# GpSimd makes the lo parts of the activations at four exchanges

## The chip, the core and the metric

The kernel runs on one core of a Trainium2 chip. Its time is that of one execution on the device, in microseconds (us). Four compute engines matter: TensorE (PE: matrix products, with PEld for its weight loads), VectorE (DVE), ScalarE (ACT) and GpSimd (POOL). SyncE (SP) issues the transfers between the chip's main memory and the on-chip memory SBUF. Results of TensorE stand in PSUM.

## The reference

One layer of a streaming encoder over 512 tokens of width 2048, all in float32:

```
h = rms_norm(x, norm_mix)
b, c, v = split(h @ conv_w_in, 3);  u = c * v
x = x + (b * conv3(u)) @ conv_w_out
h = rms_norm(x, norm_mlp)
a = relu(h @ mlp_w1)                # 2048 -> 8192
out = x + (a * a) @ mlp_w2          # 8192 -> 2048
```

The change concerns the last line, (a * a) @ mlp_w2, called the second MLP product here.

## The kernel before, in words

**Exactness.** TensorE multiplies in a shorter float format (fp32r). To keep float32 accuracy every operand is cut in two: hi is the operand rounded to fp32r, lo is the operand minus hi. A product is the sum of three: hi by hi, hi by lo, lo by hi (lines 267 to 269). `split` (lines 118 to 121) makes the parts: ScalarE copies to hi, VectorE subtracts to get lo.

**Fewer products.** Nearly all products run through `fast` (line 243), a scheme with seven products of half-size blocks instead of eight (Strassen's scheme in Winograd's form). The weights of a block of 256 output columns are cut into four quarters, from which VectorE makes four sums (line 179). The activations are likewise held as seven forms: quarters Y11, Y12 or T1, Y21, Y22 in `quart`, two of the sums T2 and T4 in `sums`, and T3 in `last_sum`. Each form is 128 partitions by 2048 elements in its hi and in its lo part.

**Steps.** A block of 256 columns is seven steps, one for each product, in the order X11, S1, S2, S4, S3, X12, X22; each has 24 matmuls (8 times 3). The order of instructions on all engines is written out by hand (lines 635 to 651): in turn i come the matmuls of step i, then `out` of step i-1 (it adds the bank to the result in c: on VectorE at line 279 for S4, S3 and X12, on ScalarE at line 281 otherwise), the weight sums of step i+3, the split of the weights of step i+2 into whi and wlo (three buffers each), and last whatever `at` has put down for that turn. Every engine works through its own list in this order, and waits where something is not ready.

**The second MLP product.** The 8192 rows of mlp_w2 are taken in four chunks of 2048. For each chunk eight blocks of 256 columns are computed, and each result c is added to a running sum x_mid (`add_up`, line 357 on VectorE, two turns after the block).

**Exchanges.** A chunk has its own seven forms of the activation, computed earlier and kept in main memory as `hidden`. They have to replace the old ones in SBUF while the last block of the work before still uses them. `exchange` (lines 343 to 350) does it during that block and the next: `fetch` (line 302) loads form i into one of three buffers f (tag q), `settle` (line 305) splits f into the hi and lo part of the form. With s the block's first step, the forms are settled in turns s+2, s+3, s+4, s+6, s+9, s+10 and s+11, and first used in steps s+7 to s+13:

```
for i in range(7):
    at(start + reads[i], fetch, box, src, i)
for i, t in enumerate((2, 3, 4, 6, 9, 10, 11)):
    at(start + t, settle, box, i)
```

There are four exchanges, hence 28 calls of `settle` in them: the first in the last block of the first MLP product, where the same buffers also serve `squared_relu` (lines 193 and 435 on VectorE), the others between the chunks. `settle` is also called elsewhere, at `pass_over` and once at the end of the mixer (lines 320 to 341 and 612).

**SP's list.** All loads are issued by SyncE in the same order. Between the fetches of an exchange stand the four loads of a weight block (line 146) and the loads and stores of x_mid. A fetch that waits for a free buffer holds up what is behind it.

GpSimd has nothing to do in the whole kernel but a few constants at the start.

Of the kernel before, what the change touches and what calls it, by code (L numbers as in the profile page):

```python
# [8 lines left out]
F32 = mybir.dt.float32  # L9
# [3 lines left out]
ALU = mybir.AluOpType  # L13
# [26 lines left out]
def trunk_kernel(  # L40
# [12 lines left out]
    nc = tc.nc  # L53
    x, out = x[0], out[0]
    w_in, w_out = conv_w_in[0], conv_w_out[0]
    w1, w2 = mlp_w1[0], mlp_w2[0]
    act, dve, pe = nc.scalar, nc.vector, nc.tensor
# [49 lines left out]
    def form(i):  # L107
        if i == T3:
            return last_sum
        return [quart[n][:, HOME[i]] if i in HOME else sums[n][:, i == T4] for n in range(2)]  # L110

    def gain(which, kt):
        return par[:, which * KT + kt : which * KT + kt + 1]
# [1 line left out]
    def tap(i, kt):  # L115
        return par[:, (2 + i) * KT + kt : (2 + i) * KT + kt + 1]

    def split(hi, lo, src):

        act.copy(hi, src)  # L120
        dve.tensor_tensor(out=lo, in0=src, in1=hi.bitcast(F32), op=ALU.subtract)  # L121

    def bank():
        return psum.tile([P, S], F32, tag="acc", name="acc")
# [24 lines left out]
    def operand(src, shape):  # L149
        hi = wp.tile(shape, F32R, tag="whi", name="whi", bufs=RING)  # L150
        lo = wp.tile(shape, F32R, tag="wlo", name="wlo", bufs=RING)
        split(hi, lo, src)
        return hi, lo
# [49 lines left out]
    def at(i, fn, *args):  # L203
        between.setdefault(i, []).append((fn, args))
# [15 lines left out]
    def plain(w, r0, c0):  # L220
        box = new_block(w, r0, c0, KT // QK)

        def multiply(op, k0):
            if k0 == 0:
                box["acc"] = [bank() for _ in range(2)]
            plain_products(box["acc"], op, k0, k_first=True)

        def out(k0):
            if k0 == KT - QK:
                c = tile_c(box)  # L230
                for j in range(2):
                    act.copy(c[:, j, :], box["acc"][j])

        for k0 in range(0, KT, QK):
            steps.append((
                lambda: None,
                lambda k0=k0: plain_operand(box["r"], k0),
                lambda op, k0=k0: multiply(op, k0),
                lambda k0=k0: out(k0),
            ))  # L240
        return box
# [59 lines left out]
        box[i] = tile_q("f")  # L301
        nc.sync.dma_start(box[i], src[:, :, PLACE[i], :].rearrange("k p t -> p k t"))

    def settle(box, i):
        split(*form(i), box.pop(i))

    def fetch_pairs(box, src, k, n):

# [4 lines left out]
    def settle_pairs(box, k, n):  # L313
        f = box.pop(k).rearrange("p (k q) t -> p q k t", q=4)[:, :, :n, :]
        split(*(quart[i][:, :, k : k + n, :] for i in range(2)), f)
# [4 lines left out]
    def pass_over(last, first, src):  # L320


        s, f, box = last["start"], first["start"], {}
        at(s - 2, fetch_pairs, box, src, 0, 2)
        at(s, fetch_pairs, box, src, 2, 2)
        at(s + 1, settle_pairs, box, 0, 2)
        at(s + 1, fetch_pairs, box, src, 4, 2)
        at(s + 2, settle_pairs, box, 2, 2)
        at(s + 3, settle_pairs, box, 4, 2)
        at(s + 3, fetch_pairs, box, src, 6, 1)  # L330
        at(f, settle_pairs, box, 6, 1)
        at(f, settle_last, last)
        box = {}
        at(f + 1, fetch, box, src, T2)
        at(f + 2, fetch, box, src, T3)
        at(f + 3, settle, box, T2)
        at(f + 3, fetch, box, src, T1)
        at(f + 3, settle, box, T3)
        at(f + 3, fetch, box, src, T4)
        at(f + 4, settle, box, T1)  # L340
        at(f + 6, settle, box, T4)

    def exchange(start, src, reads):


        box = {}
        for i in range(7):
            at(start + reads[i], fetch, box, src, i)
        for i, t in enumerate((2, 3, 4, 6, 9, 10, 11)):
            at(start + t, settle, box, i)  # L350


    wide = lambda t: t.unsqueeze(1).to_broadcast([P, 2, S])
# [121 lines left out]
    with tc.tile_pool(name="xin", bufs=2) as xin:  # L475
# [18 lines left out]
        for c in range(D // XC):  # L494
# [5 lines left out]
            for i in range(2):  # L500
                src = w_in[c * XC : (c + 1) * XC, parts[i] : parts[i] + GC]
# [3 lines left out]
            for j in range(0, XK, 2):  # L505
                xs = xin.tile([P, 2, S], F32, tag="xs", name="xs")
                for i in range(2):
                    kt = c * XK + j + i
                    pt = bank()
                    for b in range(S // P):  # L510
# [3 lines left out]
                    hi, lo = (quart[n][:, 2 * i : 2 * i + 2, kt // 2, :] for n in range(2))  # L514
# [3 lines left out]
                        out=lo, in0=pt, scalar=gain(0, kt), in1=hi.bitcast(F32),  # L518
# [83 lines left out]
    for n in range(NG):  # L602
        if n in (0, NG - 1):
            box = plain(w_out, 0, n * GC)
        else:
            box = fast(w_out, 0, n * GC, late=n == 1)
# [9 lines left out]
    for n in range(DFF // GC):  # L616
        last, box = box, fast(w1, 0, n * GC, late=n == 1) if n else plain(w1, 0, n * GC)
        if n == 0:
            pass_over(last, box, normed)
            at(box["start"] + 2, token_factors, lambda name: tile_x(name)[:, 0, :S])  # L620
        if n == DFF // GC - 1:
            exchange(box["start"], hidden[0], (-2, -1, 2, 3, 4, 5, 6))
        squared_relu(n, box)
    for ch in range(NCH):
        if ch:
            exchange(box["start"], hidden[ch], (-2, -1, 0, 2, 3, 4, 6))
        for n in range(NG):
            box = fast(w2, ch * D, n * GC)
            add_up(ch, n, box)
# [52 lines left out]
```

## Time and profile before

| what | us |
|---|---|
| median of 3 runs (lowest, highest) | 2005.88 (2002.95, 2007.34) |
| the profiled execution's own time | 2005.84 |
| its span, first to last instruction | 2004.1 |
| TensorE busy in the span | 1932.6 |
| VectorE busy | 1650.9 |
| ScalarE busy | 979.5 |
| GpSimd busy | 0.7 |

The mean granted clock of TensorE is 0.985 of full speed. Matmuls overlap, so that TensorE's busy time says only where it rests. A group row of the profile reads: line, engine, operation, output<-inputs, shapes, count, then the busy time in us, the mean ns of one, and the idle time of the engine just before them with what ended it. A timeline row reads: start in us from the span's start, length in us, engine, line, operation, operands, and in brackets the idle time before it with what released it.

### The profile page before, as it was taken

What the parts mean: (1) busy time and instruction counts of PE and PEld (TensorE: products, weight loads), DVE (VectorE), ACT (ScalarE), POOL (GpSimd) and SP (SyncE); (2) the same over time, 40 slices, a digit from 0 to 9 for tenths busy, and PEclk for the clock granted to TensorE, in tenths of its full rate; (3) what the DMA queues carried; (4) which work ended last, traced back from release to release, by engine and by line L of the source; (5) the groups of instructions that cost most, each with busy time, mean ns of one, the idle gap of its engine ahead of it and who ended that gap; (6) DMA issues with size and microseconds to landing.
All of it is one profiled execution on the core that took longest, in us unless ns stands there. A gap on an engine that the chain in (4) does not pass through costs nothing. (4 is left out here: it accounts for less than half of the span.)

```text
span 2004.1 us, 36810 instructions
## 1 busy us (share of the span) xinstructions
PE 1932.6 (96%) x15729; PEld 1886.7 (94%) x15729; DVE 1650.9 (82%) x1686; ACT 979.5 (49%) x1232; POOL 0.7 (0%) x6
## 2 busy tenths in 40 slices
PE   9979999999989989999999999988999999999998
PEld 7769999999789879999999999988998998999998
DVE  6678988887688778888888888888889789879776
ACT  4544444444455544444544445454455446446443
POOL 0000000000000000000000000000000000000000
PEclk9999999999989989999999999999999999999999
DMA  8433433434755855445354453575556457548432
GB/s 273 168 126 112 142 130 103 148 106 170 266 184 198 306 177 171 152 165 180 136 190 152 164 181 135 190 250 177 183 198 243 159 188 265 178 149 291 161 136 96
DMA packets 279843, 355.79 MB, mean 178 GB/s; under 512 B 9520, under 2 KB 253312, under 8 KB 273536
## 3 DMA queue, kind: packets, MB, share of 16 engines
q1 hardware_dynamic: 279552, 353.41, 50.8%
q8 instruction: 123, 2.02, 0.4%
q14 instruction: 40, 0.33, 0.0%
q10 hardware_dynamic: 128, 0.04, 0.0%
HBM read 277.91 MB, written 75.50 MB: 176 GB/s over the span
## 5 line engine op out<-in xcount | busy, mean ns | idle before, releaser
L267 PE MATMUL acc<-q_hi,whi 128*128 128x256 f32 x2816 | 781.3, 277 | 4.0 <-ACT c L281 4.0
L269 PE MATMUL acc<-q_hi,wlo 128*128 128x256 f32 x2816 | 780.2, 277 | 2.6 <-DVE wlo L121 2.6
L268 PE MATMUL acc<-q_lo,whi 128*128 128x256 f32 x2816 | 780.5, 277 | 1.0 <-DVE q_lo L121 1.0
L121 DVE TENSOR_TENSOR wlo<-r,whi 128x1024 fp32r<-128x1024 f32 x384 | 469.2, 1222 | 232.2 <-ACT whi L120 222.6
L267 PEld LDWEIGHTS acc<-q_hi,whi 128*128 128x128 f32 x2816 | 531.1, 189 | 4.3 <-ACT c L281 4.2
L269 PEld LDWEIGHTS acc<-q_hi,wlo 128*128 128x128 f32 x2816 | 530.1, 188 | 3.1 <-DVE wlo L121 3.0
L268 PEld LDWEIGHTS acc<-q_lo,whi 128*128 128x128 f32 x2816 | 530.6, 188 | 1.9 <-DVE q_lo L121 1.8
L120 ACT CAST whi<-r 128x1024 fp32r<-128x1024 f32 x384 | 401.0, 1053 | 212.6 <-PE acc L268 115.8
L267 PE MATMUL acc<-t_hi,whi 128*128 128x256 f32 x1408 | 397.4, 282 | 32.8 <-DVE c L279 21.8
L269 PE MATMUL acc<-t_hi,wlo 128*128 128x256 f32 x1408 | 395.6, 281 | 2.2 <-DVE wlo L121 2.2
L268 PE MATMUL acc<-t_lo,whi 128*128 128x256 f32 x1408 | 395.5, 281 | 0.0
L120 ACT CAST whi<-s 128x1024 fp32r<-128x1024 f32 x264 | 278.4, 1055 | 206.0 <-DVE s L179 143.6
L121 DVE TENSOR_TENSOR wlo<-s,whi 128x1024 fp32r<-128x1024 f32 x264 | 322.3, 1221 | 25.9 <-ACT whi L120 22.2
L281 ACT COPY c<-acc 128x256 f32<-128x256 f32 x352 | 130.3, 370 | 402.2 <-PE acc L269 386.7
L267 PEld LDWEIGHTS acc<-t_hi,whi 128*128 128x128 f32 x1408 | 271.4, 193 | 35.1 <-issue 23.3
L269 PEld LDWEIGHTS acc<-t_hi,wlo 128*128 128x128 f32 x1408 | 270.9, 192 | 2.4 <-DVE wlo L121 2.4
L268 PEld LDWEIGHTS acc<-t_lo,whi 128*128 128x128 f32 x1408 | 271.1, 193 | 0.0
L267 PE MATMUL acc<-u_hi,whi 128*128 128x256 f32 x704 | 203.7, 289 | 13.5 <-ACT c L281 13.5
L268 PE MATMUL acc<-u_lo,whi 128*128 128x256 f32 x704 | 201.4, 286 | 1.3 <-DVE u_lo L121 1.3
L269 PE MATMUL acc<-u_hi,wlo 128*128 128x256 f32 x704 | 201.4, 286 | 0.0
L267 PEld LDWEIGHTS acc<-u_hi,whi 128*128 128x128 f32 x704 | 136.9, 195 | 14.7 <-ACT c L281 14.7
L268 PEld LDWEIGHTS acc<-u_lo,whi 128*128 128x128 f32 x704 | 137.0, 195 | 2.0 <-DVE u_lo L121 2.0
(76 smaller groups left out, 1796.7 us busy)
## 6 DMA issues: line engine op xcount, KB each, us to landing
r<-in_mlp_w_dram SPq DMA_DIRECT2D x256, 512.0 KB, 6.2
r<-in_conv_w_in_dram SPq DMA_DIRECT2D x96, 512.0 KB, 6.2
hidden<-q SPq DMA_DIRECT2D x32, 1024.0 KB, 4.3
f<-hidden SPq DMA_DIRECT2D x28, 1024.0 KB, 8.4
r<-in_conv_w_out_dram SPq DMA_DIRECT2D x32, 512.0 KB, 6.4
xt<-x_mid SPq DMA_DIRECT2D x32, 512.0 KB, 8.8
x_mid<-c SPq DMA_DIRECT2D x24, 512.0 KB, 2.6
gated<-q SPq DMA_DIRECT2D x8, 1024.0 KB, 3.8
```

Source lines behind the costliest of these rows:

```text
L120: act.copy(hi, src)
L121: dve.tensor_tensor(out=lo, in0=src, in1=hi.bitcast(F32), op=ALU.subtract)
L267: pe.matmul(acc, hi[:, k, :], f_hi[:, k, :], start=first, stop=False, skip_group_check=True)
L268: pe.matmul(acc, hi[:, k, :], f_lo[:, k, :], start=False, stop=False, skip_group_check=True)
L269: pe.matmul(acc, lo[:, k, :], f_hi[:, k, :], start=False, stop=last, skip_group_check=True)
L281: act.copy(o, acc)
```

## The change

`split` gets an argument that names the engine of the subtraction, VectorE where nothing is said; `settle` passes it on; and `exchange`, alone of the callers, passes GpSimd. ScalarE's copy to hi stays, the fetches stay, and so do all turns.

```diff
-    def split(hi, lo, src):
+    def split(hi, lo, src, rest=dve):
 
         act.copy(hi, src)
-        dve.tensor_tensor(out=lo, in0=src, in1=hi.bitcast(F32), op=ALU.subtract)
+        rest.tensor_tensor(out=lo, in0=src, in1=hi.bitcast(F32), op=ALU.subtract)
...
-    def settle(box, i):
-        split(*form(i), box.pop(i))
+    def settle(box, i, rest=dve):
+        split(*form(i), box.pop(i), rest)
...
         for i, t in enumerate((2, 3, 4, 6, 9, 10, 11)):
-            at(start + t, settle, box, i)
+            at(start + t, settle, box, i, nc.gpsimd)
```

The 28 subtractions of 128 by 2048 elements leave VectorE's list and form GpSimd's. The buffer f is free again when GpSimd's subtraction has ended, and TensorE's products with the lo part wait for GpSimd.

## The prediction

> **What bounds the kernel now.** I read the page first, for which engine is full, then stretches of the span, to compare the exchanges with ordinary work, and then the groups, the timeline and the DMA issues inside one exchange.
>
> ```profile
> PE 1932.6 (96%) x15729; PEld 1886.7 (94%) x15729; DVE 1650.9 (82%) x1686; ACT 979.5 (49%) x1232; POOL 0.7 (0%) x6
> ```
>
> TensorE is the bound of the whole; VectorE (DVE) is next. Below, columns are: length, busy time (count) of PE, PEld, DVE, ACT, POOL, granted clock, DMA share, GB/s.
>
> ```profile
> 1799.00:1818.10 19.10, 19.10 (x169) 19.10 (x168) 15.34 (x16) 9.64 (x12) 0.00 (x0) 1.00 0.77 267
> 1829.00:1833.30 4.30, 4.30 (x24) 4.30 (x25) 4.30 (x5) 2.86 (x2) 0.00 (x0) 0.63 1.09 387
> ```
>
> The first row is an ordinary stretch, about one block of seven steps: TensorE never rests, DVE needs 15.34 of 19.10 us, GpSimd does nothing. The second is explained below.
>
> ```profile
> 1322.00:1369.00 47.00, 33.86 (x248) 32.89 (x247) 38.75 (x35) 26.07 (x24) 0.00 (x0) 0.88 0.71 241
> 1493.00:1534.00 41.00, 36.32 (x295) 35.58 (x295) 39.22 (x33) 26.73 (x26) 0.00 (x0) 0.96 0.84 291
> 1654.00:1695.00 41.00, 36.62 (x300) 35.88 (x299) 39.47 (x33) 26.61 (x26) 0.00 (x0) 0.96 0.84 292
> 1815.00:1856.00 41.00, 36.96 (x298) 36.22 (x298) 39.44 (x33) 26.76 (x26) 0.00 (x0) 0.96 0.84 291
> ```
>
> These hold the four exchanges. TensorE is idle 13.1, 4.7, 4.4 and 4.0 us of them, and DVE is nearly full in the last three, which are alike. I work with the fourth. Its DVE groups, from the first lo part to the last (1819.30 to 1852.05):
>
> ```profile
> L121 DVE TENSOR_TENSOR q_lo<-f,q_hi 128x2048 fp32r<-128x2048 f32 x4 | 9.1, 2284 | 0.0
> L121 DVE TENSOR_TENSOR wlo<-r,whi 128x1024 fp32r<-128x1024 f32 x6 | 7.3, 1218 | 0.1
> L121 DVE TENSOR_TENSOR t_lo<-f,t_hi 128x2048 fp32r<-128x2048 f32 x2 | 4.6, 2284 | 0.0
> L121 DVE TENSOR_TENSOR wlo<-s,whi 128x1024 fp32r<-128x1024 f32 x3 | 3.7, 1219 | 0.0
> L357 DVE TENSOR_TENSOR c<-c,xt 128x1024 f32<-128x1024 f32 x2 | 2.4, 1219 | 0.0
> L121 DVE TENSOR_TENSOR u_lo<-f,u_hi 128x2048 fp32r<-128x2048 f32 x1 | 2.3, 2284 | 0.0
> L279 DVE TENSOR_TENSOR c<-acc,c 128x256 f32<-128x256 f32 x5 | 2.1, 417 | 0.0
> L179 DVE TENSOR_TENSOR r<-r 128x1024 f32<-128x1024 f32 x1 | 1.2, 1218 | 0.0
> L179 DVE TENSOR_TENSOR s<-r,s 128x1024 f32<-128x1024 f32 x1 | 1.2, 1217 | 0.0
> L179 DVE TENSOR_TENSOR s<-s,r 128x1024 f32<-128x1024 f32 x1 | 1.2, 1216 | 0.0
> L179 DVE TENSOR_TENSOR s<-r 128x1024 f32<-128x1024 f32 x1 | 1.2, 1215 | 0.0
> ```
>
> Idle before them is 0.1 us in all: DVE sets the pace for these 33 us. The timeline shows that instructions overlap by some 0.08 us, and what TensorE waits for:
>
> ```profile
> 1819.23 2.29 DVE L121 TENSOR_TENSOR q_lo<-f,q_hi 128x2048 fp32r<-128x2048 f32 x1
> 1821.43 1.22 DVE L121 TENSOR_TENSOR wlo<-r,whi 128x1024 fp32r<-128x1024 f32 x1
> 1822.57 2.29 DVE L121 TENSOR_TENSOR q_lo<-f,q_hi 128x2048 fp32r<-128x2048 f32 x1
> ...
> 1849.83 2.28 DVE L121 TENSOR_TENSOR t_lo<-f,t_hi 128x2048 fp32r<-128x2048 f32 x1
> 1852.03 0.42 DVE L279 TENSOR_TENSOR c<-acc,c 128x256 f32<-128x256 f32 x1
> ```
> ```profile
> 1829.00 0.55 PE L267 MATMUL acc<-t_hi,whi 128*128 128x256 f32 x1 [2.40 <-DVE c L279]
> 1852.59 0.36 PE L267 MATMUL acc<-t_hi,whi 128*128 128x256 f32 x1 [1.20 <-DVE c L279]
> ```
>
> Start to start, a lo part takes 2.20 us of DVE (1819.23 to 1821.43), a weight operand 1.14 (1821.43 to 1822.57). Twice TensorE stands because the short addition of line 279 sits behind a lo part. After the 2.40 us gap the clock is down: 0.63 over 4.30 us in the row above, so 4.30 x 0.37 = 1.6 us more.
>
> **The change, part by part.** *Removed from DVE:* 28 lo parts, seven per exchange, 7 x 2.20 = 15.4 us each time, with DVE the pace. If nothing came in their place, the fourth exchange would need 32.8 - 15.4 = 17.4 us of DVE, less than TensorE's own work there, and the losses would go.
>
> *Added to GpSimd:* the same 28, 128x2048 with two inputs from SBUF. No row shows one. The nearest:
>
> ```profile
> masks.py:199 POOL TENSOR_SCALAR_AFFINE_SELECT ident<-ident 128x128 f32<-128x128 f32 x1 | 0.3, 292 | 0.1
> ...
> L668 POOL MEMSET const-float32-0.0<- 128x1 f32 x1 | 0.1, 98 | 0.2 <-issue 0.2
> ```
>
> With 98 ns fixed, one tensor read costs GpSimd (292 - 98)/128 = 1.52 ns an element, so 2048 take 3.2 us with one input and, if the inputs are read in turn, 6.3 with two. Below, DVE's 2.3 is the floor. I take X = 4.7, between one and two inputs, and keep 3.2 and 6.3. The Trainium skill, GPSIMD Engine Reference, section 3.1, states 4497 ns for just this operation at this size; the sum would then be 2059 us; no run shows it yet.
>
> *What hides it.* Seven in a row on GpSimd take 7 x 4.7 = 32.9 us, from the end of the first hi part on:
>
> ```profile
> 1816.81 1.91 ACT L120 CAST q_hi<-f 128x2048 fp32r<-128x2048 f32 x1
> ...
> 1848.10 1.05 ACT L120 CAST whi<-r 128x1024 fp32r<-128x1024 f32 x1
> ```
>
> That is 1818.7 to 1851.6, against 1852.1 for the last lo part now. So even with DVE untouched the last lo part comes hardly earlier: the chain moves from DVE to GpSimd, which lags behind the steps set for a DVE twice as fast. Behind a waiting GpSimd instruction only further lo parts are queued, and TensorE waits for them.
>
> *Moved: the release of f.* Three buffers serve seven fetches, and the fourth fetch starts as the first lo part ends:
>
> ```profile
> 1821.54 0.36 SPq L302 DMA_DIRECT2D f<-hidden  x1
> ...
> 1828.96 4.61 SPq L146 DMA_DIRECT2D r<-in_mlp_w_dram  x4
> ```
> ```profile
> f<-hidden SPq DMA_DIRECT2D x4, 1024.0 KB, 6.7
> r<-in_mlp_w_dram SPq DMA_DIRECT2D x8, 512.0 KB, 7.8
> ```
>
> Landing 6.7, hi part 1.9 and lo part 4.7 make 13.3 us for three, under GpSimd's own 14.1: the fetches stay hidden. Behind the sixth fetch on SP's queue stand four weight loads; the third release moves from 1828.5 to 1818.7 + 14.1 = 1832.8, so they move 4.3 us. They end their issue at 1833.6 and land by 1841.4, first used at 1848.1: 6.7 us of room, cost nothing. If GpSimd is still slower, that room goes too, but then all else is late as well.
>
> *Unknown: what DVE loses while GpSimd reads.* No row has both at work. The ends: nothing, or DVE's instructions with two SBUF inputs stand as long as GpSimd runs. In the fourth exchange those are 9 weight lo parts, 2 of line 357 and the 4 sums, less the one that overlaps the start (line 357 before 1819.23): 14 x 1.14 = 16.0 us. At the upper end 16.0 + 32.9 = 48.9 us take the place of 32.8 (line 279 reads PSUM and fits in between): +16.1. The point of balance is near half: 16.0 + 5 x 0.34 + 7 x 2.2 = 33.1. Anything above 2.2 us of standing per lo part loses, and nothing below it wins more than GpSimd's own chain allows. I take the upper end, because loss grows from there while the gain is capped. The Trainium skill, SBUF — State Buffer, section on the two separate sides, says that GpSimd and a VectorE instruction with two SBUF inputs take one pair of ports in turn, each for a whole instruction; by that rule the upper end holds, and without it the sum is that of the second rival. No row here shows the one or the other.
>
> *First exchange.* Its DVE groups from 1326.70 to 1367.90, those that differ:
>
> ```profile
> L121 DVE TENSOR_TENSOR wlo<-r,whi 128x1024 fp32r<-128x1024 f32 x6 | 7.3, 1220 | 3.2 <-ACT whi L120 3.2
> L121 DVE TENSOR_TENSOR wlo<-s,whi 128x1024 fp32r<-128x1024 f32 x3 | 3.7, 1220 | 0.0
> ...
> L193 DVE TENSOR_TENSOR q<-q 128x256 f32<-128x256 f32 x4 | 1.7, 424 | 0.1
> ...
> L193 DVE TENSOR_TENSOR q<-q 128x512 f32<-128x512 f32 x2 | 1.4, 686 | 0.0
> ...
> L435 DVE SCALAR_TENSOR_TENSOR c<-c,rbc 128x1024 f32<-128x1024 f32 x1 | 1.2, 1218 | 0.0
> ```
>
> 9 + 1 + 4 sums = 14 x 1.14 = 16.0, and 3.1 of line 193: 19.1 + 32.9 = 52.0 us against 41.2 now, idle time included: +10.8.
>
> *Sum.* 3 x 16.1 + 10.8 = 59.1 us. The lowered clock I leave as it is (0 to 4 x 1.6 = 6.4 more): TensorE would work about 2.7 of every 7 us there and doesn't set the pace. The profiled execution took 2005.84 us (span 2004.1), beside a median of 2005.88: **2065 us**.
>
> **Rivals.** *1, forecast: DVE stands.* 2065; with X from 3.2 to 6.3 it is 2005.84 + 3 x 5.6 + 0.3 = 2023 to 2005.84 + 3 x 27.3 + 22.0 = 2110. For it: DVE packed, both inputs of nearly all its work in SBUF. Against: no overlap of the two was ever recorded. *2, GpSimd's chain alone.* DVE is untouched, but 7 x 4.7 = 32.9 us replace 32.8. The wait on line 279 goes (up to 0.9 us at the end of each of three exchanges, 2.7), and with it perhaps four times 1.6 us of low clock: 1997 to 2003, say 2000. *3, the other side: GpSimd is fast enough.* If X is 3.2 and DVE doesn't stand, a hi part ends some 0.4 + 1.0 + 1.9 = 3.3 us into its step, the lo part 6.5, against the two steps (2 x 19.10 / 7 = 5.5) that the last three have: 1.0 us late at the fifth, 0.4 more at each of the next two. So of the fourth exchange's loss (4.0 idle and 1.6 of clock) 1.8 us stays: 3 x 3.8 = 11 gained, and of the first's 13.1, where f is also late, about half: 6 to 8. With the clock of the first (0.88 over 47 us, 5.6 us) half restored, 3: 21 in all, 1985 us. It decides from X below 4 with less than 2.2 us of standing. For it: the page shows GpSimd wholly free; against: even the one-input row scales to 3.2. *4, DVE is slowed, not stopped:* a third to two thirds of the 59 us, 2025.
>
> **How the numbers follow.** Forecast 0.50, second rival 0.21, third 0.16, fourth 0.13. About 0.2% (4 us) can be told from no change. Faster: all of the third and 0.12 of the second, 0.28. Same: the rest of the second, 0.09. Slower: 0.63. The range 1985 to 2085 leaves out half of the third (0.08) and the forecast's slow end with X above 5.5 (0.10); the forecast's own range is 2023 to 2110.
>
> **What would show it.** In the changed profile GpSimd has 28 instructions of line 121; X is read from consecutive ones. The step on standing is right if weight lo parts on DVE last or wait several microseconds beside them and TensorE waits for wlo or for GpSimd's lo parts; it is wrong if they stay at 1.22 us and DVE shows idle time. The f fetches should come later by X less 2.2 per release. The prediction fails if the exchanges get shorter than 41 us, or if GpSimd needs under 3.2 us.

## The result and the profile after

The changed kernel takes 2064.88 us (median of three, 2064.18 to 2064.88) against 2005.88: 1.03 times the time before, 95% interval 1.0285 to 1.0314, slower by 59 us. The forecast was 2065. Part of that closeness is luck, as the terms below show.

The page of the changed kernel, engines and their busy time; then its GpSimd groups:

```profile
span 2063.1 us, 36852 instructions
...
PE 1952.5 (95%) x15729; PEld 1903.7 (92%) x15729; DVE 1698.0 (82%) x1658; ACT 979.2 (47%) x1232; POOL 147.2 (7%) x34
```
```profile
L121 POOL TENSOR_TENSOR q_lo<-f,q_hi 128x2048 fp32r<-128x2048 f32 x16 | 84.2, 5276 | 1736.8 <-ACT q_hi L120 1732.6
L121 POOL TENSOR_TENSOR t_lo<-f,t_hi 128x2048 fp32r<-128x2048 f32 x8 | 43.0, 5374 | 1.5 <-ACT t_hi L120 1.5
L121 POOL TENSOR_TENSOR u_lo<-f,u_hi 128x2048 fp32r<-128x2048 f32 x4 | 19.7, 4922 | 25.6 <-ACT u_hi L120 25.6
```

VectorE gave away 28 instructions, 28 x 2.20 = 61.6 us, and is busy 47.1 us *longer* (1698.0 against 1650.9). So the instructions that it kept grew by 108.7 us. Where they grew is seen in its groups in the fourth exchange (1864.3 to 1911.6):

```profile
L121 DVE TENSOR_TENSOR wlo<-r,whi 128x1024 fp32r<-128x1024 f32 x6 | 22.4, 3730 | 1.9 <-ACT whi L120 1.8
L179 DVE TENSOR_TENSOR s<-r 128x1024 f32<-128x1024 f32 x2 | 10.6, 5299 | 0.0
L179 DVE TENSOR_TENSOR s<-r,s 128x1024 f32<-128x1024 f32 x1 | 5.5, 5535 | 0.0
L121 DVE TENSOR_TENSOR wlo<-s,whi 128x1024 fp32r<-128x1024 f32 x3 | 3.6, 1213 | 0.0
L279 DVE TENSOR_TENSOR c<-acc,c 128x256 f32<-128x256 f32 x5 | 2.1, 411 | 0.0
L357 DVE TENSOR_TENSOR c<-c,xt 128x1024 f32<-128x1024 f32 x1 | 1.2, 1217 | 0.0
L179 DVE TENSOR_TENSOR r<-r 128x1024 f32<-128x1024 f32 x1 | 1.2, 1212 | 0.0
L179 DVE TENSOR_TENSOR s<-s,r 128x1024 f32<-128x1024 f32 x1 | 1.2, 1210 | 0.0
```

Instructions of one kind now last 1.2 or some 5.3 us. The timelines of the two engines, VectorE first, tell when (GpSimd's first row holds two instructions):

```profile
1863.01 1.22 DVE L357 TENSOR_TENSOR c<-c,xt 128x1024 f32<-128x1024 f32 x1
1864.90 4.97 DVE L121 TENSOR_TENSOR wlo<-r,whi 128x1024 fp32r<-128x1024 f32 x1 [0.67 <-ACT whi L120]
1869.79 0.41 DVE L279 TENSOR_TENSOR c<-acc,c 128x256 f32<-128x256 f32 x1
1870.12 5.31 DVE L121 TENSOR_TENSOR wlo<-r,whi 128x1024 fp32r<-128x1024 f32 x1
1875.36 0.41 DVE L279 TENSOR_TENSOR c<-acc,c 128x256 f32<-128x256 f32 x1
1875.70 5.28 DVE L179 TENSOR_TENSOR s<-r 128x1024 f32<-128x1024 f32 x1
1880.90 1.21 DVE L121 TENSOR_TENSOR wlo<-r,whi 128x1024 fp32r<-128x1024 f32 x1
```
```profile
1863.73 10.63 POOL L121 TENSOR_TENSOR q_lo<-f,q_hi 128x2048 fp32r<-128x2048 f32 x2 [128.30 <-ACT q_hi L120]
1874.32 5.58 POOL L121 TENSOR_TENSOR t_lo<-f,t_hi 128x2048 fp32r<-128x2048 f32 x1
1884.02 5.18 POOL L121 TENSOR_TENSOR q_lo<-f,q_hi 128x2048 fp32r<-128x2048 f32 x1 [4.12 <-ACT q_hi L120]
```

While GpSimd works, one VectorE instruction with two SBUF inputs lasts to the end of GpSimd's and 1.1 us beyond; then the turn is GpSimd's again, and its next one starts its own wait behind that VectorE instruction. The two go in turn. Line 279, which reads PSUM and one SBUF tensor, runs its usual 0.41 us at 1869.79, in the midst of a GpSimd instruction. In the fourth exchange seven lo parts on GpSimd hold up seven VectorE instructions, one each.

What TensorE waits for, in the changed kernel from 1300 us on:

```profile
PE acc L267 <- DVE c L279: 19.8, 5, 7.7
PE acc L269 <- DVE wlo L121: 17.7, 10, 3.6
PE acc L268 <- POOL q_lo L121: 8.1, 4, 2.4
PE acc L267 <- ACT c L281: 6.5, 2, 4.9
PE acc L268 <- POOL u_lo L121: 5.9, 3, 2.1
PE acc L268 <- POOL t_lo L121: 4.6, 3, 2.5
```

The wait for line 279 was there before (19.7 us). New are 17.7 us for the lo parts of weights, which are held up themselves or stand in VectorE's list behind held-up instructions, and 18.6 us for GpSimd itself. The stretches that hold the four exchanges (columns as in the prediction):

```profile
1322.00:1384.00 62.00, 40.81 (x273) 39.46 (x272) 50.48 (x30) 27.48 (x26) 34.20 (x7) 0.80 0.55 189
1507.00:1565.00 58.00, 44.77 (x323) 43.30 (x322) 54.22 (x29) 28.24 (x28) 37.28 (x7) 0.88 0.68 232
1683.00:1741.00 58.00, 42.98 (x311) 41.50 (x310) 54.83 (x28) 27.44 (x27) 37.54 (x7) 0.88 0.66 226
1858.00:1916.00 58.00, 44.76 (x323) 43.29 (x323) 54.25 (x28) 28.39 (x29) 37.44 (x7) 0.88 0.69 234
```

TensorE is idle 21.2, 13.2, 15.0 and 13.2 us there, 62.6 against 26.2 before. Besides, the granted clock is 0.80 and 0.88 where it was 0.88 and 0.96: length times what is missing gives about 33 us against 11. In TensorE's account the loss is thus some 36 us of standing and some 20 of slow clock (22 by that product, which also counts slow stretches in which TensorE stands). A slow stretch follows a gap:

```profile
1875.92 0.55 PE L267 MATMUL acc<-t_hi,whi 128*128 128x256 f32 x1 [3.21 <-DVE c L279]
1876.27 0.41 PE L268 MATMUL acc<-t_lo,whi 128*128 128x256 f32 x1
```

Matmuls that lasted 0.28 us ahead of the gap last 0.41, and from 1876.2 to 1881.6 the granted clock is 0.50. So the slow clock is taken here as a consequence of the gaps; that is read from the order in time and was not tested by itself.

Not all of the 59 us lies in the exchanges. A step ahead of the first of them, where both kernels are the same, starts in the kernel before and in the changed one at

```profile
1305.91 0.33 PE L267 MATMUL acc<-u_hi,whi 128*128 128x256 f32 x1
```
```profile
1308.76 0.32 PE L267 MATMUL acc<-u_hi,whi 128*128 128x256 f32 x1
```

so 2.9 us arose ahead of the exchanges, and about 56 belong to them. In the profiled executions of all ten kernels, which are alike up to there, that step starts between 1303.6 and 1308.8 us: 2.9 us is scatter of single executions.

### The profile page after: what moved, and what is told of

Same layout as the page of the kernel before. It is cut to its first block, busy times and chain, and to the rows that moved or that the text cites. A ratio compares the mean times of both kernels' runs of the same rounds, so it can differ in the third digit from the quotient of the medians.

```text
span 2063.1 us, 36852 instructions
## 1 busy us (share of the span) xinstructions
PE 1952.5 (95%) x15729; PEld 1903.7 (92%) x15729; DVE 1698.0 (82%) x1658; ACT 979.2 (47%) x1232; POOL 147.2 (7%) x34
## 5 line engine op out<-in xcount | busy, mean ns | idle before, releaser
L121 DVE TENSOR_TENSOR wlo<-r,whi 128x1024 fp32r<-128x1024 f32 x384 | 522.2, 1360 | 247.5 <-ACT whi L120 237.7
L269 PEld LDWEIGHTS acc<-q_hi,wlo 128*128 128x128 f32 x2816 | 533.8, 190 | 13.8 <-DVE wlo L121 13.8
L121 POOL TENSOR_TENSOR q_lo<-f,q_hi 128x2048 fp32r<-128x2048 f32 x16 | 84.2, 5276 | 1736.8 <-ACT q_hi L120 1732.6
```

The lines of the kernel that those rows point to most:

```text
L121: rest.tensor_tensor(out=lo, in0=src, in1=hi.bitcast(F32), op=ALU.subtract)
L269: pe.matmul(acc, lo[:, k, :], f_hi[:, k, :], start=False, stop=last, skip_group_check=True)
```

## The experiments

Each is one kernel, compared with the kernel before on the same chip. "Theory" is the forecast's: VectorE stands while GpSimd reads.

**GpSimd works beside VectorE, and nobody waits for it.**

```diff
+    def beside(i):
+        hi = form(i)[0].bitcast(F32)
+        spare = ssq.rearrange("p (k t) -> p k t", k=2)
+        for k in range(0, NP, 2):
+            part = hi[:, k : k + 2, :]
+            nc.gpsimd.tensor_tensor(out=spare, in0=part, in1=part, op=ALU.subtract)
...
             at(start + t, settle, box, i)
+            at(start + t, beside, i)
```

> VectorE makes all lo parts as before; beside each, GpSimd subtracts a form's hi part from itself in four pieces of 128x512, into a spare tile that nobody reads (extra work, the result is unchanged). Theory (VectorE's instructions with two SBUF inputs stand while GpSimd reads): 7 x 4.5 = 31.5 us of standing per exchange come on top of the 32.8 us of VectorE, some of it taken up by idle time after the exchange: 2090 to 2130 us, and VectorE's two-input instructions last 1.2 us or more longer beside each piece. Rival (GpSimd is only slow, and what costs is that TensorE and the fetches wait for its results): nobody waits for these, so 2006 us and VectorE's instructions unchanged at 1.22 and 2.28 us.

Measured 2078.65 us against 2005.72, ratio 1.0369 (1.0339 to 1.0399): 73 us slower, though no engine needs a result of GpSimd; that is below the range of the theory. The page, and one instruction of each engine:

```profile
PE 1955.4 (94%) x15729; PEld 1905.1 (92%) x15729; DVE 1732.8 (83%) x1686; ACT 979.9 (47%) x1232; POOL 236.3 (11%) x118
```
```profile
1898.62 2.06 DVE L121 TENSOR_TENSOR wlo<-s,whi 128x1024 fp32r<-128x1024 f32 x1
```
```profile
1899.67 1.90 POOL L348 TENSOR_TENSOR ssq<-q_hi 128x512 f32<-128x512 f32 x1
```

VectorE has the same instructions as before and is busy 81.9 us longer; a weight lo part of 1.22 us lasts 2.06 beside a piece. This shows the standing by itself, and rules out that the slow results of GpSimd are the whole cost. The size was overrated: a piece costs this instruction 0.84 us; four of them would be 3.4 and not 4.5, and on average it is 81.9 / 28 = 2.9.

**GpSimd copies, with one input.** The same with this in the loop:

```diff
+            nc.gpsimd.tensor_copy(out=spare, in_=hi[:, k : k + 2, :])
```

> As the run with GpSimd beside VectorE, but GpSimd copies the hi part (one input) in four pieces. Theory, if any reading by GpSimd makes VectorE stand: 2 to 3.2 us per form by the one-input row (1.52 ns an element), so 4 x 7 x 2 to 3.2 us = 56 to 90, less idle time: 2045 to 2095 us. If only two inputs collide with two inputs: 2006 us.

Measured 2032.24 us, ratio 1.0137 (1.0108 to 1.0167): 27 us slower.

```profile
PE 1938.4 (95%) x15729; PEld 1890.2 (93%) x15729; DVE 1685.2 (83%) x1686; ACT 980.4 (48%) x1232; POOL 190.7 (9%) x118
```
```profile
1839.08 2.70 DVE L121 TENSOR_TENSOR q_lo<-f,q_hi 128x2048 fp32r<-128x2048 f32 x1
1841.71 1.63 DVE L121 TENSOR_TENSOR wlo<-r,whi 128x1024 fp32r<-128x1024 f32 x1
```

One input makes VectorE stand too, but only 0.41 us a piece here (1.63 against 1.22), so the time lies below the range that was worked out from the one-input row.

**GpSimd only writes.** VectorE makes the lo part; then GpSimd fills the used buffer twice.

```diff
+    def fill(box, i):
+        f = settle(box, i)
+        for _ in range(2):
+            nc.gpsimd.memset(f, 0.0)
...
-            at(start + t, settle, box, i)
+            at(start + t, fill, box, i)
```

> VectorE makes all lo parts as before; after each, GpSimd fills the used buffer f with zeros twice (128x2048, writes only), which holds the buffer back by about 2 x 1.8 us as the slow subtraction does. Theory (GpSimd's reading is what collides): VectorE's instructions keep 1.22 us and the time stays at 2004 to 2012 us, the buffers being a little late. Rival (anything GpSimd does in SBUF makes VectorE stand): 7 x 3.6 = 25 us per exchange, 2070 to 2100 us. Rival (the late buffers are the cost of the change): 2040 us or more.

Measured 2010.06 us against 2005.72, ratio 1.0022 (1.0006 to 1.0038).

```profile
PE 1930.8 (96%) x15729; PEld 1884.5 (94%) x15729; DVE 1650.0 (82%) x1686; ACT 980.6 (49%) x1232; POOL 101.5 (5%) x62
```
```profile
L348 POOL MEMSET f<- 128x2048 f32 x56 | 100.8, 1813 | 1760.8 <-DVE q_lo L121 1731.2 <-DVE u_lo L121 21.9 <-DVE t_lo L121 6.1
```

101 us of GpSimd add nothing to VectorE (1650.0 against 1650.9): writing doesn't collide. Holding each buffer back by 3.6 us costs some 4 us in all, so the later release of f is a small part of the change's cost at most. In the profiled execution it lies in the first exchange alone: its eleven steps take TensorE 56.3 us in place of 50.2, while the other three exchanges come out within 0.6 us of before. There the buffers also serve `squared_relu`, and ScalarE waits 6.1 us for one that is being filled, where it waited 3.6 for VectorE; in the changed kernel it waits 5.0 us for the one of u_lo at that place.

**The forms settled as early as possible,** GpSimd still making all lo parts.

```diff
-        for i, t in enumerate((2, 3, 4, 6, 9, 10, 11)):
+        for i, t in enumerate((2, 3, 4, 5, 6, 7, 8)):
```

> The changed kernel, with the forms settled as early as their old contents allow, in turns 2, 3, 4, 5, 6, 7 and 8 in place of 2, 3, 4, 6, 9, 10 and 11, so that GpSimd has up to three more steps (8 us) for the last ones. Theory (VectorE stands): as many instructions of VectorE are held up for as long, 2045 to 2070 us. Rival (GpSimd's results come too late for their steps): TensorE's waits for lo parts go and the time falls to 2010 us or below.

Measured 2073.24 us, ratio 1.0342 (1.0312 to 1.0372), somewhat above the range and slower than the changed kernel. TensorE's waits from 1300 us on:

```profile
PE acc L269 <- DVE wlo L121: 58.0, 16, 7.8
PE acc L267 <- DVE c L279: 9.7, 3, 3.2
PE acc L267 <- ACT q_hi L120: 7.8, 1, 7.8
```

No wait for GpSimd is left, and still nothing is won: the waits moved to the weight lo parts. Lateness of GpSimd's results alone is thus not what sets the time. That the seven, closer together, hold VectorE up more densely is the likely reason for the longer time; no run separates it from the rest of the new order.

**One of the seven.**

```diff
-            at(start + t, settle, box, i, nc.gpsimd)
+            at(start + t, settle, box, i, nc.gpsimd if i == Y22 else dve)
```

> GpSimd makes one of the seven lo parts (Y22, turn 6), VectorE the other six. Theory (each GpSimd lo part holds one or two VectorE instructions up for 4.5 us or so, in place of 2.2 us of VectorE's own): 4 x (4.5 - 2.2) = 9 us more, up to 14 with waiting: 2012 to 2020 us. Rival (VectorE is relieved and GpSimd's chain of seven is the cost): 4 x 2.2 = 9 us less, 1997 us.

Measured 2013.35 us against 2004.96, ratio 1.0046 (1.0029 to 1.0064): 8.4 us.

```profile
PE 1931.3 (96%) x15729; PEld 1884.7 (94%) x15729; DVE 1659.1 (83%) x1682; ACT 979.9 (49%) x1232; POOL 21.7 (1%) x10
```
```profile
1838.79 5.60 DVE L179 TENSOR_TENSOR s<-r,s 128x1024 f32<-128x1024 f32 x1
```

The price of one lo part, cleanly: a sum of 1.22 us lasts 5.60, so 4.4 us of standing in place of 2.2 of work, four times 2.2 = 8.7. VectorE is busy 8.2 us longer. Relief of VectorE, the rival, would have shown 9 us less.

**Each lo part in four pieces.**

```diff
-        rest.tensor_tensor(out=lo, in0=src, in1=hi.bitcast(F32), op=ALU.subtract)
+        if rest is dve:
+            dve.tensor_tensor(out=lo, in0=src, in1=hi.bitcast(F32), op=ALU.subtract)
+        else:
+            for k in range(0, NP, 2):
+                p = slice(k, k + 2)
+                rest.tensor_tensor(out=lo[:, p], in0=src[:, p], in1=hi.bitcast(F32)[:, p], op=ALU.subtract)
```

> The changed kernel with each lo part made in four GpSimd instructions of 128x512. Theory (the sum of both engines' reading time sets the pace): the sum is the same, so 2050 to 2075 us, with VectorE's instructions held up some 1.2 us each and more of them. Rival (what costs is that one long instruction keeps an urgent VectorE instruction waiting): VectorE gets in between, 2035 us or less.

Measured 2075.29 us, ratio 1.0355 (1.0325 to 1.0384), 0.3 us above the range and 10 us above the changed kernel.

```profile
PE 1966.0 (95%) x15729; PEld 1905.8 (92%) x15729; DVE 1667.3 (80%) x1658; ACT 979.7 (47%) x1232; POOL 212.7 (10%) x118
```
```profile
PE acc L273 <- POOL q_lo L126: 16.4, 24, 1.3
PE acc L273 <- POOL t_lo L126: 16.1, 25, 1.3
PE acc L274 <- DVE wlo L122: 9.3, 9, 1.5
```

VectorE stands less, 1667.3 - 1650.9 + 61.6 = 78 us against 108.7, but 79 of the 112 pieces first wait for a VectorE instruction (most of these last 2.2 to 2.3 us, the others 1.3), so GpSimd needs 212.7 us, and TensorE now waits 36 us for its lo parts (16.4, 16.1 and 3.7 for u_lo). That one long instruction keeps an urgent one waiting is not what makes the change slow; the sum of both engines' reading alone doesn't give the time either.

**VectorE's list less crowded,** without GpSimd. The second of the two kernels has the moved additions alone.

```diff
-        for i, t in enumerate((2, 3, 4, 6, 9, 10, 11)):
+        for i, t in enumerate((2, 3, 5, 6, 9, 10, 11)):
...
-        at(box["end"] + 2, product)
+        d = {NG - 2: 1, NG - 1: 6}.get(n, 2) if ch < NCH - 1 else 2
+        at(box["end"] + d, product)
         if ch < NCH - 1:
-            at(box["end"] + 3, lambda: nc.sync.dma_start(x_mid[ch + 1][n], flat(box["c"])))
+            at(box["end"] + d + 1, lambda: nc.sync.dma_start(x_mid[ch + 1][n], flat(box["c"])))
```

> The kernel before, VectorE for all lo parts, with VectorE's list in the exchange made less crowded: the third form is settled in turn 5 in place of 4, and between chunks the addition to x_mid of the last but one block comes one turn earlier, that of the last block four turns later. If VectorE's pace in the exchange is the loss, 2 x 1.14 us are taken out of three exchanges (7 us) and the gap of 2.4 us with its 1.6 us of lowered clock gets shorter: 1993 to 2001 us. If TensorE's gaps come from something else: 2006 us.

> As the less crowded kernel, but the third form stays in turn 4: the additions to x_mid alone are moved. 3 x 2 x 1.14 = 7 us less if VectorE sets the pace throughout: 1997 to 2002 us.

Measured 2002.21 us against 2004.96, ratio 0.9991 (0.9981 to 1.0002), and 2005.11, ratio 0.9998 (0.9986 to 1.001): no difference that can be told, and both above the ranges that VectorE's pace would have given. With the additions moved alone, the timeline shows where the gain went:

```profile
1497.96 2.29 DVE L121 TENSOR_TENSOR q_lo<-f,q_hi 128x2048 fp32r<-128x2048 f32 x1 [0.58 <-ACT q_hi L120]
...
1535.48 1.21 DVE L357 TENSOR_TENSOR c<-c,xt 128x1024 f32<-128x1024 f32 x1
```

Where the addition stood, VectorE now waits for ScalarE's hi part (0.58 us), and the late one comes at 1535.48, when VectorE has still not caught up. The additions had filled time that is worth little. None of these kernels beats the kernel before by a measurable amount.

## Why the prediction was right, point by point

*Removed from VectorE:* the 61.6 us went as reckoned, and were taken back nearly twice, by 108.7 us of standing.

*GpSimd's duration, X = 4.7:* the shortest of the 28 takes 4.51 us, and 5.6 us when a VectorE instruction of 1.1 stands in front, a wait that the prediction did not have. The Trainium skill's figure for a `tensor_tensor` of this size (GPSIMD Engine Reference, section 3.1: 4497 ns, for an addition) agrees with the shortest, a subtraction, within 0.3%.

*What DVE loses, the upper end:* right in kind, and too large in size. In the run with one of seven VectorE stands 4.4 us for a lo part, and in the changed kernel 108.7 / 28 = 3.9 on average, where 4.7 were taken. The Trainium skill's rule (SBUF — State Buffer, on the two separate sides) holds in the runs: VectorE instructions with two SBUF inputs stand behind a GpSimd instruction that reads (5.3 against 1.2 us) and not behind one that writes only, and one that reads PSUM passes (0.41 us). The timelines show besides that the engines go in turn where both have work.

*The fourth exchange:* forecast 16.0 + 32.9 = 48.9 us from the first lo part to the last; measured, 1863.73 to 1911.66, where GpSimd's last one ends:

```profile
1906.05 5.61 POOL L121 TENSOR_TENSOR t_lo<-f,t_hi 128x2048 fp32r<-128x2048 f32 x1
```

47.9 us, against 32.8 before. The forecast's form of the sum holds: VectorE's own work of 16.0 us and seven times the 4.51 us that GpSimd needs by itself make 47.6. In VectorE's list this shows as 45.7 us of instructions with two SBUF inputs (the groups above without line 279), the last of which ends 1.1 us after GpSimd's, and 1.9 us of waiting for ScalarE.

*GpSimd's chain:* forecast 32.9 us without a break. It is busy 37.4 (the row from 1858) and has to wait 4.1 and 6.4 us for hi parts in between, since the steps themselves are late. Its lo parts are late for TensorE as well, 18.6 us over all exchanges: the second rival's mechanism is there, as a part. The early run shows that taking it away wins nothing.

*The release of f and the weight loads:* the direction was right. In SP's timeline the fourth fetch comes as the first lo part ends, and the weight loads follow:

```profile
1868.81 0.37 SPq L302 DMA_DIRECT2D f<-hidden  x1
...
1880.34 3.53 SPq L146 DMA_DIRECT2D r<-in_mlp_w_dram  x4
```

From the first lo part's start the loads come 16.6 us later, where it was 9.7 (1819.23 to 1828.96): 6.9 us of delay, not 4.3, because each lo part took 5.1 to 5.6 us. From the first exchange on no engine of the changed kernel waits for a weight load, so the forecast's nothing holds for them. For the first exchange it doesn't: there the run that only fills loses 6 us by late buffers.

*The lowered clock, taken as unchanged:* a term whose size was wrong. By the windows it takes about 33 us of full-speed work from TensorE against 11, outside the 0 to 6.4 that was allowed. How much of it is on the path can't be settled, since TensorE at half speed (0.50 in the stretch above) partly fills time in which it would have waited anyway. VectorE is busy 47 us longer, and the exchanges grew by 56; in the other 9 us VectorE stands idle. Whether these come from the slow clock, from the waits for GpSimd or from late buffers no run separates.

*Why the total fits, in part by luck:* with the measured 4.51 in place of 4.7, the forecast's own sum is 14.8 us for each of the last three exchanges and 9.5 for the first, 54 in all. Measured are 13.8, 15.7 and 14.1, and 12.6 for the first. So the duration was 5 us too large over 28 lo parts, the first exchange some 3 too small, and another 3 us lie ahead of the exchanges, where the change does nothing. That these cancel is what put 2065 beside 2064.88.

*The first exchange:* forecast +10.8, measured by TensorE's steps +12.6 (50.2 us for eleven steps before, 1322.46 to 1372.64, and 62.8 after, 1325.30 to 1388.05); the others +13.8 to +15.7 where 16.1 was forecast.

*Rivals:* the third, GpSimd fast enough, fell with X = 4.5 and with the standing; the fourth, VectorE slowed and not stopped, with the rows in which it waits out the whole instruction.

## What to carry to other kernels

In this kernel work moved from VectorE to GpSimd was no relief, because VectorE's instructions meanwhile read two SBUF tensors. A subtraction that cost VectorE 2.2 us cost it 3.9 to 4.4 us on GpSimd. Before such a move, count the two-input instructions on VectorE's list in the stretch, and set GpSimd's duration against that of the removed work as if both engines were one. Where GpSimd only writes, or VectorE reads PSUM, the two went side by side.

## What the runs showed of the hardware that was not expected

The engines take turns: in each of the last three exchanges seven GpSimd instructions hold up exactly seven VectorE instructions, and with both lists full each is itself held up by one (5.6 us in place of 4.51). So cutting GpSimd's work into four pieces does not let it slip through; it hands VectorE more turns, and the lo part gets late (GpSimd busy 212.7 us in place of 147.2). A GpSimd copy with one input holds VectorE up too, 0.41 us for 128x512 against 0.84 with two inputs. And a fill of 128x2048 takes GpSimd 1.81 us and VectorE nothing.
